# TensorE's order through two attention branches, written by hand in place of the planner's

## The chip, the cores and the metric

The kernel runs on one NeuronCore of a Trainium2 chip. The metric is device time in microseconds, from the first to the last instruction of one launch with what lies around it; the median of three runs is given. TensorE does the matrix products, VectorE, ScalarE and GpSimd (POOL in the rows) the elementwise work, and SyncE (SP) issues most DMAs.

## The reference, cut to what matters

Two layers of a decoder trunk over 1024 tokens of width 1024. In each layer one input projection of the normalised x feeds three branches, whose gated sum goes through an output projection.

```python
h = _rms(x, norm_g[l])
proj = h @ w_in[l]
# differential attention: 4 heads, two score maps of 64 each, causal
q = _partial_rope(_rms(q.reshape(B, S, DA_HEADS, 2, DA_QK_DIM), q_g), cos, sin)
k = _partial_rope(_rms(k.reshape(B, S, DA_HEADS, 2, DA_QK_DIM), k_g), cos, sin)
p = jax.nn.softmax(sc, axis=-1)
wdiff = p[:, :, 0] - lam * p[:, :, 1]
o = _rms(o, subln_g) * (1.0 - lam_init)          # o = wdiff @ v, then * silu(z)
# recurrent branch (RWKV-7): a scan over time
# memory cross-attention: 4 heads of 128, 256 memory tokens, softmax(q km) vm * silu(z)
gates = jax.nn.sigmoid(gate_logits.reshape(B, S, N_BRANCH, D_MODEL))
merged = jnp.sum(gates * branch_proj, axis=2)
x = x + merged @ w_out[l]
```

## The kernel before

Activations lie transposed, channels on partitions and tokens on the free axis. The input projection is cut into 65 column tiles of 128 channels a layer. A tile is two halves of 512 tokens; a half is 24 matmuls (8 blocks of the contraction, three products each, since weights and activations are split into a high and a low part). `project` (L220) computes one tile: `weight` (L198) loads 512 KB on SP's queue, ScalarE makes the high part, GpSimd the low part; then, for each half, 24 matmuls into a tile of the pool `pj` (two buffers) and a function `take` that reads it out. Work that needs TensorE again, such as sums over channels, is put on a list by `put_off` and runs when the next half has been taken; `run_later` empties the list at once.

The stages of a layer follow one another: the projections of the recurrent branch; its scan (`rwkv_run`), in which TensorE's order is written by hand and the tiles of a list (16 gate tiles and 8 SiLU tiles) are put in between by `fill`; cross attention; differential attention; merge; output projection. In the two attentions the order on every engine is a planner's, which goes by its own costs and by the order of the program. There `cross_prepare` (L818) projects the queries of the next head while `cross_run` (L838) runs one, and `diff_prepare` (L879) projects k, q and v of the next head (norm, spread of the norm over the tokens, rotation) while `diff_run` (L935) runs one. `FC` and `FD` say behind which heads a gate tile is projected (one in cross attention, one after each of the four heads of the other); one more follows. That makes 22 of 24 gate tiles, which are stored to `g_d` and loaded again in `merge`; `merge` projects the other two itself.

A head of differential attention goes through eight tiles of 128 queries. `scores(t)` makes both score maps in the pool `pg` (three buffers), takes the maximum on VectorE and the exponential on ScalarE, which frees the buffer; `finish(t)`, one tile later, combines the two maps on VectorE, transposes the result through the pool `pa` (tag "a", two buffers), copies it out and multiplies it with v. At the end `ov` is normalised and transposed once more. The sums, the spread norm (`ps_rb`) and v's transposes go through the pool `pu` (one buffer). The ring `dsn` has two buffers, which the rotation of k and q and the copy of v (L924) share.

Lines of helpers in the profile: L171 and L174 are VectorE's or GpSimd's two-operand operations, L178 ScalarE's high part, L214 every matmul of `project`, L249 a transpose, L269 the token sums in three parts ("sq", "rest").

Of the kernel before, what the change touches and what calls it, by code (L numbers as in the profile page):

```python
# [19 lines left out]
P = 128  # L20
# [36 lines left out]
FC, FD = (0, 1, 0, 0), (1, 1, 1, 1)  # L57

F_0, F_INV, F_H, F_U, F_S, F_END = 40, 140, (18, 8), 7, 6, (72, 72)
EARLY = 16  # L60
# [3 lines left out]
LAG = 1  # L64
# [66 lines left out]
def trunk(ctx, tc, io, out, layers=DEPTH, dump=None):  # L131
# [89 lines left out]
    def project(h, l, j, take, eng=None):  # L221
        w = weight(io["w_in"][l, j], eng)
        for hf in range(2):
            ps = pj.tile([P, 512], F32, name="ps_pj", tag="pj")
            product(ps, w, h, NK, slice(0, P), half(hf))
            old = later[:]
            later.clear()
            take(hf, ps)
            new = later[:]
            later.clear()  # L230
            for n, then in old:
                if n > 1:
                    later.append((n - 1, then))
                else:
                    then()
            later.extend(new)

    later = []

# [18 lines left out]
    def token_sums3(mp, ss, sq, rhs, bufs=2, eng=None):  # L258
# [6 lines left out]
        def sums(first):  # L265
# [7 lines left out]
    def spread(ps, col, n, c):  # L273
# [3 lines left out]
        nc.scalar.copy(bv, col.rearrange("p (j c) -> p j c", c=c).unsqueeze(3).to_broadcast([P, n, c, P // c]))  # L277
        for j in range(n):
            transpose(ps[:, j * P:(j + 1) * P], b[:, j * P:(j + 1) * P])
# [165 lines left out]
    def dense(h, l, items):  # L445

        def steps():
            ahead = weight(io["w_in"][l, items[0][0]])
            for t, (j, take) in enumerate(items):
                w = ahead  # L450
                ahead = weight(io["w_in"][l, items[t + 1][0]]) if t + 1 < len(items) else None
                for hf in range(2):
                    ps = pj.tile([P, 512], F32, name="ps_pj", tag="pj")
                    n = 0
                    for k in range(NK):
                        for a, b in ((0, 0), (0, 1), (1, 0)):
# [3 lines left out]
                            if n == 3 * NK:  # L460
                                take(hf, ps)
                            yield
        return steps()
# [149 lines left out]
    def rwkv_run(l, ch, dc, sts, gen):  # L613
# [3 lines left out]

        def fill(n):
            for _ in range(n):
                next(gen, None)  # L620
# [193 lines left out]
        fill(F_END[0])  # L814
        finish(yn, 3)
        fill(F_END[1])
        for _ in gen:
            pass  # L818


    def cross_prepare(l, q, h, mp, i):
        qT = mp.tile([P, S], F32, name="cq", bufs=2)
        ss = pu.tile([P, 512], F32, name="ps_ss", tag="u")
        es = mp.tile([P, NT], F32, name="ces", bufs=2)

        def take(hf, ps):
            sq = mp.tile([P, 512], F32, name="sq", bufs=2)
            nc.scalar.copy(qT[:, half(hf)], ps)
            nc.scalar.activation(sq, ps, AF.Square)  # L829
            sums = token_sums3(mp, ss[:, hf * 4:], sq, onesb)  # L830

            def then():
                sums(hf == 0)
                if hf == 1:
                    rsqrt(es, ss[:, :NT], NT, 1.0 / P, EPS, post=P ** -0.5)
            put_off(then)
        project(h, l, T_CAQ + i, take)
        return qT, es  # L838

    def cross_run(mp, kT, vm, i, qT, es):  # L840
# [3 lines left out]
        for t2 in range(4):  # L844
            ps = pg.tile([P, 512], F32, name="ps_c", tag="g")
            for u in range(2):
                t = t2 * 2 + u
                nc.tensor.matmul(ps[:, u * M:u * M + M], qT[:, t * P:t * P + P], kT[:, i, :], start=True, stop=True)
# [4 lines left out]
            stt(mx, mx, -1.0, es[:, t2 * 2:t2 * 2 + 2], ALU.mult, ALU.mult)  # L853
            e = mp.tile([P, 2, M], F32, name="ce", bufs=2)
            for u in range(2):
                t = t2 * 2 + u
                nc.scalar.activation(e[:, u, :], pv[:, u, :], AF.Exp, scale=es[:, t:t + 1], bias=mx[:, u:u + 1],
                                     accum_out=ls[:, u:u + 1])
            nc.vector.reciprocal(ls, ls)
            for u in range(2):  # L860
                nc.vector.tensor_scalar(e[:, u, :], e[:, u, :], ls[:, u:u + 1], None, op0=ALU.mult)
            pt = pa.tile([P, 512], F32, name="ps_t", tag="a")
# [3 lines left out]
            for m in range(2):  # L866
                nc.vector.tensor_copy(pT[m][:, t2 * 256:t2 * 256 + 256], pt[:, m * 256:m * 256 + 256])
        for hf in range(2):
# [3 lines left out]
            y = mp.tile([P, 512], F32, name="ce", bufs=2)  # L872
            ttv(y, ps, zs[:, half(hf)], ALU.mult)
            nc.gpsimd.dma_start(y_d[2, i][:, half(hf)], y)
        run_later()


    def diff_prepare(l, q, h, mp, rope, i):

        cos, sin, rot = rope  # L880
        es = mp.tile([P, NT, 2], F32, name="des", bufs=2)
        qk = {}

        def rest(n, g, ss):
            if n == "q":
                rsqrt(es.rearrange("p t c -> p (t c)"), ss[:, :16], 16, 1.0 / 64, EPS, post=0.125)
            else:
                r = mp.tile([P, 16], F32, name="dkr", bufs=2)
                rsqrt(r, ss[:, :16], 16, 1.0 / 64, EPS)
                for hf in range(2):  # L890
                    rb = pu.tile([P, 512], F32, name="ps_rb", tag="u")
                    spread(rb, r[:, hf * 8:hf * 8 + 8], 4, 2)
                    ttv(g[:, half(hf)], g[:, half(hf)], rb, ALU.mult)
# [9 lines left out]
        for n, tl in (("k", T_DAK), ("q", T_DAQ)):  # L903
            g = mp.tile([P, S], F32, name="d" + n, bufs=1)
            ss = pu.tile([P, 512], F32, name="ps_ss", tag="u")

            def take(hf, ps, n=n, g=g, ss=ss):
# [3 lines left out]
                sums = token_sums3(mp, ss[:, hf * 8:], sq, hindb)  # L911

                def then():
                    sums(hf == 0)
                    if hf == 1:
                        rest(n, g, ss)
                put_off(then)
            project(h, l, tl + i, take)
            qk[n] = g
        v = mp.tile([P, NT, P], F32, name="dv", bufs=2)  # L920

        def take_v(hf, ps):
# [3 lines left out]
            def then(vt=vt):  # L926
                pt = pu.tile([P, 512], F32, name="ps_t", tag="u")
                for j in range(4):
                    transpose(pt[:, j * P:j * P + P], vt[:, j * P:j * P + P])
                nc.scalar.copy(v[:, hf * 4:hf * 4 + 4, :].rearrange("p t d -> p (t d)"), pt)  # L930
            put_off(then)
        project(h, l, T_DAV + i, take_v)
        return qk, v, es

    def diff_run(l, q, te, mp, identb, negb, kl, i, qk, v, es, beside):  # L935
# [19 lines left out]
        def scores(t):  # L955
# [3 lines left out]
            for c in range(2):  # L959
# [18 lines left out]
                stt(mx[:, 0:1], mx[:, 0:1], -1.0, es[:, t, c:c + 1], ALU.mult, ALU.mult)  # L978
                e = mp.tile([P, S], F32, name="de", bufs=4)
# [9 lines left out]
        def finish(t, ee, ll):  # L989
# [9 lines left out]
            for b in range(nb):  # L999
# [17 lines left out]
        for t in range(NT):  # L1017
            pend.append((t, *scores(t)))
            if len(pend) > LAG:
                finish(*pend.pop(0))  # L1020
            if t == 2:
                run_later()
        for u in pend:
            finish(*u)
        beside()
# [125 lines left out]
    for l in range(layers):  # L1151
# [4 lines left out]
        def fill(n):  # L1156
            for _ in range(n):
                g = queue.pop(0)
                early.add(g)
                project(h, l, T_GATE + g[0] * 8 + g[1], take_gate(*g))  # L1160
        with tc.tile_pool(name="st", bufs=1) as sp:
# [14 lines left out]

            silus = [(T_CAZ + i, take_silu(2, i)) for i in range(4)] + [(T_DAZ + i, take_silu(0, i)) for i in range(4)]
            items = []
            for i in range(EARLY):
# [71 lines left out]
```

## Time and profile before

| | us |
|---|---|
| median of the runs | 2776.12 |
| lowest and highest of 3 runs | 2769.37, 2777.94 |
| profiled execution, its own time | 2769.06 |
| its span, first to last instruction | 2767.3 |

The rows below come from that one profiled execution. Times in rows are in us; names are those of the program, out<-in. A number in brackets at the end of a row of the timeline is how long the engine sat idle before it, and what ended that. The granted clock (PEclk) is 1.00 when TensorE has its full rate.

### The profile page before, as it was taken

To read this page: it belongs to the slowest core of one execution; us is meant where nothing else is said; L and a number is where in the kernel's file an instruction comes from. 1 tells how busy PE (TensorE), PEld (TensorE's weight loads), DVE (VectorE), ACT (ScalarE), POOL (GpSimd) and SP (SyncE) were. 2 spreads that over 40 slices of the span, in tenths; PEclk is the share of its full clock that TensorE was granted. 3 is DMA by queue.
4 is the path that set the end of the run, shared out by engine and by line. 5 is a ranking of instruction groups with operands and counts; after the bars stand their busy time and mean duration, and the time that the engine had idled before them with its cause. 6 is when DMAs were issued, how large, how long until landed. Compare 5 with 4: busy or idle time off the path is not lost. (4 is left out here: it accounts for less than half of the span.)

```text
span 2767.3 us, 40395 instructions
## 1 busy us (share of the span) xinstructions
PE 2643.5 (96%) x15686; PEld 2144.8 (78%) x15686; DVE 1690.4 (61%) x3427; ACT 986.6 (36%) x1927; POOL 816.0 (29%) x716
## 2 busy tenths in 40 slices
PE   7799999999999999999999999999999999999999
PEld 7788788888876777777877778888887677777787
DVE  3748557557356777845556765656735577774552
ACT  4444322212232555722234432222223345573221
POOL 3445522232312222122234652123231222212210
PEclk8799999999999999999999999999999999999999
DMA  4323442322322112155352345223232211114534
GB/s 156 105 92 122 149 146 96 104 88 64 117 75 77 39 54 58 50 182 165 118 163 75 115 133 180 88 85 101 79 106 81 80 43 54 51 53 171 171 108 150
DMA packets 94479, 286.91 MB, mean 104 GB/s; under 512 B 12368, under 2 KB 19152, under 8 KB 91856
## 3 DMA queue, kind: packets, MB, share of 16 engines
q1 hardware_dynamic: 67088, 196.24, 23.5%
q0 software_dynamic: 25024, 83.90, 7.8%
q10 hardware_dynamic: 2176, 4.19, 0.4%
q8 instruction: 123, 2.02, 0.3%
q14 instruction: 68, 0.56, 0.1%
HBM read 198.31 MB, written 83.89 MB: 102 GB/s over the span
## 5 line engine op out<-in xcount | busy, mean ns | idle before, releaser
L171 POOL TENSOR_TENSOR w_lo<-w_raw,w_hi 128x1024 fp32r<-128x1024 f32 x170 | 421.2, 2478 | 937.5 <-ACT w_hi L178 891.1
L214 PE MATMUL ps_pj<-hh,w_hi 128*128 128x512 f32 x1568 | 634.5, 405 | 1.2 <-ACT hh L178 1.2
L214 PE MATMUL ps_pj<-hl,w_hi 128*128 128x512 f32 x1568 | 625.6, 399 | 1.2 <-DVE hl L171 1.2
L214 PE MATMUL ps_pj<-hh,w_lo 128*128 128x512 f32 x1568 | 622.9, 397 | 0.6 <-DVE w_lo L171 0.6
L178 ACT ACTIVATE w_hi<-w_raw 128x1024 fp32r<-128x1024 f32 x202 | 213.9, 1059 | 670.4 <-PE ps_pj L214 242.9
L214 PEld LDWEIGHTS ps_pj<-hl,w_hi 128*128 128x128 f32 x1568 | 298.1, 190 | 62.4 <-issue 4.3
L214 PEld LDWEIGHTS ps_pj<-hh,w_lo 128*128 128x128 f32 x1568 | 297.9, 190 | 61.7 <-issue 1.4
L214 PEld LDWEIGHTS ps_pj<-hh,w_hi 128*128 128x128 f32 x1568 | 297.7, 190 | 61.1 <-issue 2.9
L457 PE MATMUL ps_pj<-hh,w_hi 128*128 128x512 f32 x768 | 308.1, 401 | 0.0
L457 PE MATMUL ps_pj<-hl,w_hi 128*128 128x512 f32 x768 | 306.4, 399 | 0.0
L457 PE MATMUL ps_pj<-hh,w_lo 128*128 128x512 f32 x768 | 304.9, 397 | 0.0
L457 PEld LDWEIGHTS ps_pj<-hh,w_hi 128*128 128x128 f32 x768 | 146.5, 191 | 30.5
L457 PEld LDWEIGHTS ps_pj<-hh,w_lo 128*128 128x128 f32 x768 | 146.3, 190 | 30.4
L457 PEld LDWEIGHTS ps_pj<-hl,w_hi 128*128 128x128 f32 x768 | 146.5, 191 | 29.4
L1080 PE MATMUL ps_b<-yh,w_hi 128*128 128x512 f32 x384 | 147.5, 395 | 9.5 <-ACT yh L178 9.5
L1080 PE MATMUL ps_b<-yl,w_hi 128*128 128x512 f32 x384 | 152.7, 400 | 2.3 <-DVE misc L342 1.2
L1080 PE MATMUL ps_b<-yh,w_lo 128*128 128x512 f32 x384 | 150.5, 395 | 0.0
L981 ACT ACTIVATE de<-ps_d,dmx,des 128x512 f32<-128x512 f32 (+2 forms) x192 | 127.7, 670 | 50.7 <-DVE dmx L174 44.1
L171 DVE TENSOR_TENSOR rest<-sq 128x512 f32<-128x512 f32 x48 | 65.7, 1369 | 111.5 <-ACT sq L829 82.2
L974 DVE TENSOR_REDUCE dmx<-ps_d 128x1 f32<-128x512 f32 (+2 forms) x192 | 103.9, 551 | 23.1 <-PE ps_d L973 19.6
L442 POOL DMA_DIRECT2D g_d<-z_t x88 | 49.0, 557 | 213.3 <-ACT z_t L441 130.0
L171 DVE TENSOR_TENSOR inv_u<-inv_l,inv_x 128x126 f32<-128x126 f32 (+22 forms) x248 | 96.3, 388 | 16.4 <-ACT inv_l L670 9.6
(297 smaller groups left out, 4507.3 us busy)
## 6 DMA issues: line engine op xcount, KB each, us to landing
w_raw<-in_w_in_dram SPq DMA_DIRECT2D x130, 512.0 KB
g_d<-z_t POOLq DMA_DIRECT2D x88, 256.0 KB, 4.7
tg<-g_d SPq DMA_DIRECT2D x88, 256.0 KB
w_raw<-in_w_out_dram SPq DMA_DIRECT2D x32, 512.0 KB
z_d<-z_t POOLq DMA_DIRECT2D x48, 256.0 KB, 3.0
w_raw<-in_w_branch_dram SPq DMA_DIRECT2D x24, 512.0 KB
yr<-y_d SPq DMA_DIRECT2D x24, 512.0 KB
w_raw<-in_w_mem_dram SPq DMA_DIRECT2D x16, 512.0 KB
```

The costliest lines, as they stand in the source:

```text
L171: (eng or nc.vector).tensor_tensor(o, a, b, op=op)
L178: nc.scalar.activation(hi, src, AF.Copy)
L214: nc.tensor.matmul(ps, w[a][:, k, cols], act[b][:, k, toks], start=n == 0, stop=n == 3 * nk - 1)
L442: nc.gpsimd.dma_start(g_d[n, d][:, half(hf)], tg)
L457: nc.tensor.matmul(ps, w[a][:, k, :], h[b][:, k, half(hf)], start=n == 0, stop=n == 3 * NK - 1)
L974: nc.vector.tensor_reduce(mx[:, b:b + 1], ps[:, :n], axis=AX.X, op=ALU.max)
L981: nc.scalar.activation(e[:, b * 512:b * 512 + n], ps[:, :n], AF.Exp, scale=es[:, t, c:c + 1], bias=mx[:, 0:1], accum_out=ls[:, b:b + 1])
L1080: nc.tensor.matmul(pb, wb[a][:, i, (d % 2) * P:(d % 2) * P + P], b[i][:, half(hf)], start=k3 == 0, stop=k3 == 11)
```

## The change

In both attentions TensorE's order is now the program's. One list of column tiles (`Dense`) goes through the scan, cross attention and differential attention; `fill(n)` issues the next n matmuls of the list, up to a limit, and `until` issues all up to a tile. The constants say how many stand behind each step: `C_S`, `C_T`, `C_E` in cross attention, `D_S`, `D_M`, `D_T`, `D_E` in the other. The token sums, the spread of k's norm and v's transposes run when the next half tile has been taken. The queries of cross attention are projected two heads ahead; k, q, v and one gate tile of the next head lie inside each head of differential attention (192 matmuls), two gate tiles inside the last one, whose fills are halved. The spread norm and v's transposes move from `pu` to `pa`. The scan has 15 gate tiles instead of 16, 23 gates are early instead of 22, and the last fills of the scan are 60 and then what is left.

```diff
-F_0, F_INV, F_H, F_U, F_S, F_END = 40, 140, (18, 8), 7, 6, (72, 72)
-EARLY = 16
+F_0, F_INV, F_H, F_U, F_S, F_END = 40, 140, (18, 8), 7, 6, 60
+EARLY = 15
+C_S, C_T, C_E = 7, 3, 6
+D_S, D_M, D_T, D_E = (6, 8, 8, 10, 8, 8, 8, 8), (12, 6), 3, (12, 20)
...
+    class Dense:
+        def __init__(self, h, l):
+            self.items, self.done, self.limit, self.gen = [], 0, 0, self.steps(h, l)
...
+            for t, (j, take) in enumerate(self.items):
+                w = ahead or weight(io["w_in"][l, j])
+                ahead = weight(io["w_in"][l, self.items[t + 1][0]]) if t + 1 < len(self.items) else None
...
                             if n == 3 * NK:
-                                take(hf, ps)
+                                taken(take, hf, ps)
+                                self.done = t + hf
                             yield
...
+        def fill(self, n):
+            for _ in range(n):
+                if self.done < self.limit:
+                    next(self.gen)
+
+        def until(self, n):
+            while self.done < n:
+                next(self.gen)
...
+        ee = []
+        for t2 in range(4):
+            ee.append(scores(t2))
+            fill(C_S)
+            if t2:
+                turn(t2 - 1, ee[t2 - 1])
+                fill(C_T)
+        fill(C_E)
+        turn(3, ee[3])
+        fill(C_E)
...
+                bs = [spread_by_tokens(r[:, hf * 8:hf * 8 + 8], 4, 2) for hf in range(2)]
+
+                def then():
+                    for hf in range(2):
+                        rb = pa.tile([P, 512], F32, name="ps_rb", tag="a")
+                        for j in range(4):
+                            transpose(rb[:, j * P:(j + 1) * P], bs[hf][:, j * P:(j + 1) * P])
+                        ttv(g[:, half(hf)], g[:, half(hf)], rb, ALU.mult)
+                    rotate(n)
+                put_off(then)
...
-            def then(vt=vt):
-                pt = pu.tile([P, 512], F32, name="ps_t", tag="u")
+            def then():
+                pt = pa.tile([P, 512], F32, name="ps_t", tag="a")
...
                     last = b == nb - 1
+                    if c and b:
+                        fill(D_M[1])
...
+                if c == 0 and nb == 2:
+                    fill(D_M[0])
                 e = mp.tile([P, S], F32, name="de", bufs=4)
...
+            fill(D_T)
             po = pa.tile([P, 512], F32, name="ps_o", tag="a")
...
             pend.append((t, *scores(t)))
-            if len(pend) > LAG:
+            fill(D_S[t])
+            if t:
                 finish(*pend.pop(0))
...
+        fill(D_E[0])
+        finish(*pend.pop(0))
         rsqrt(oss, oss, NT, 1.0 / P, EPS, tag="ds")
         ttv(ov, ov, oss.unsqueeze(2).to_broadcast([P, NT, P]), ALU.mult)
+        fill(D_E[1])
...
+            unit = prepare_head(0)
+            dense.until(n_da[0])
+            for i in range(4):
+                ahead = prepare_head(i + 1) if i < 3 else None
+                dense.limit = n_da[i + 1]
+                diff_run(l, q, te, mp, identb, negb, kl, i, unit, dense.fill if i < 3 else lambda n: dense.fill(n // 2))
+                dense.until(n_da[i + 1])
+                unit = ahead
             run_later()
```

## Rows read from the trace of the kernel before

**Rows 1.** The page, part 1: busy time, share and instructions.

```profile
PE 2643.5 (96%) x15686; PEld 2144.8 (78%) x15686; DVE 1690.4 (61%) x3427; ACT 986.6 (36%) x1927; POOL 816.0 (29%) x716
```

**Rows 2.** Windows, differential attention: us; PE, PEld, DVE, ACT, POOL busy; PEclk; DMA; GB/s.

```profile
868.00:942.00 74.00, 66.91 (x362) 51.97 (x363) 44.50 (x90) 26.42 (x45) 24.09 (x15) 0.93 0.22 64
942.00:1200.00 258.00, 247.95 (x1430) 194.62 (x1429) 199.24 (x557) 155.90 (x405) 53.48 (x39) 0.99 0.19 59
...
2186.00:2262.00 76.00, 67.69 (x383) 52.29 (x381) 46.05 (x92) 28.40 (x46) 26.67 (x17) 0.98 0.22 67
2262.00:2516.00 254.00, 245.22 (x1401) 192.56 (x1402) 195.95 (x549) 152.61 (x400) 50.07 (x38) 0.97 0.18 55
```

**Rows 3.** TensorE's waits, 868:942 and 2186:2262: total us, times, longest.

```profile
PE ps_t L249 <- ACT dsn L924: 4.8, 3, 3.0
PE ps_ss L269 <- ACT sq L910: 2.6, 1, 2.6
...
PE ps_t L249 <- ACT dsn L924: 4.3, 3, 3.0
```

**Rows 4.** TensorE's waits, 740:868 (the first row stands in both layers).

```profile
PE ps_ss L269 <- DVE rest L171: 3.5, 4, 0.9
PE ps_t L249 <- DVE ce L861: 1.6, 1, 1.6
```

**Rows 5.** TensorE's waits, 942:1200 and 2262:2516.

```profile
PE ps_d L968 <- ACT de L981: 6.3, 4, 2.0
PE ps_t L249 <- ACT dsn L924: 1.8, 3, 0.6
...
PE ps_d L968 <- ACT de L981: 5.9, 3, 2.0
PE ps_t L249 <- ACT dsn L924: 1.5, 2, 0.9
```

**Rows 6.** Timeline of TensorE: start, duration; first and last of two streams.

```profile
795.54 0.40 PE L214 MATMUL ps_pj<-hl,w_hi 128*128 128x512 f32 x1
...
801.22 0.39 PE L214 MATMUL ps_pj<-hh,w_lo 128*128 128x512 f32 x1
...
873.96 0.63 PE L214 MATMUL ps_pj<-hh,w_lo 128*128 128x512 f32 x1
...
877.37 0.55 PE L214 MATMUL ps_pj<-hl,w_hi 128*128 128x512 f32 x1
```

**Rows 7.** Timeline, all engines, start of the first layer's first head.

```profile
942.77 2.36 POOL L171 TENSOR_TENSOR w_lo<-w_raw,w_hi 128x1024 fp32r<-128x1024 f32 x1 [5.99 <-PE ps_d L973]
...
943.00 2.15 DVE L174 SCALAR_TENSOR_TENSOR dmx<-dmx,des 128x1 f32<-128x1 f32 x1
...
943.10 0.48 PE L214 MATMUL ps_pj<-hh,w_hi 128*128 128x512 f32 x1
...
945.78 0.44 PE L968 MATMUL ps_d<-dkh,dqs 128*128 128x256 f32 x1 [1.97 <-ACT de L981]
```

**Rows 8.** Timelines of TensorE and ScalarE: k's norm spread, v's copy.

```profile
884.10 0.66 PE L249 MATMUL ps_rb<-con,spread 128*128 128x128 f32 x4
...
899.11 0.59 ACT L924 COPY dsn<-ps_pj 128x512 f32<-128x512 f32 x1 [10.42 <-DVE dk L171]
```

**Rows 9.** Timeline of VectorE: a step of cross attention, maximum to scaled probabilities.

```profile
785.24 0.67 DVE L852 TENSOR_REDUCE cmx<-ps_c 128x2 f32<-128x512 f32 x1
...
788.71 0.60 DVE L861 TENSOR_SCALAR ce<-ce,cls 128x256 f32<-128x256 f32 x2
```

**Rows 10.** Timeline of TensorE: first layer's merge; second layer's last head and merge.

```profile
1208.89 0.98 PE L1080 MATMUL ps_b<-yh,w_hi 128*128 128x512 f32 x3 [1.58 <-ACT yh L178]
...
2507.87 2.05 PE L1011 MATMUL ps_o<-dv,dwT 128*128 128x128 f32 x16
...
2514.60 1.07 PE L249 MATMUL ps_t<-con,dov 128*128 128x128 f32 x8 [0.33 <-DVE dov L171]
...
2528.38 0.97 PE L1080 MATMUL ps_b<-yh,w_hi 128*128 128x512 f32 x3 [2.45 <-ACT yh L178]
```

More of the change, by code (lines that the diff above doesn't have):

```diff
@@ L225, in project, with taken @@
             product(ps, w, h, NK, slice(0, P), half(hf))
-            old = later[:]
-            later.clear()
-            take(hf, ps)
[L229 to L236, printed above, removed]
-    later = []
+            taken(take, hf, ps)
+    later = []
+    def taken(take, hf, ps):
+        old = later[:]
+        later.clear()
+        take(hf, ps)
+        new = later[:]
+        later.clear()
+        for n, then in old:
+            if n > 1:
+                later.append((n - 1, then))
+            else:
+                then()
+        later.extend(new)
     def put_off(then, n=1):
@@ L443, in take_gate, with add, steps @@
         return take
[L445 to L451, printed above, removed]
+    class Dense:
+        def __init__(self, h, l):
+            self.items, self.done, self.limit, self.gen = [], 0, 0, self.steps(h, l)
+        def add(self, j, take):
+            self.items.append((j, take))
+            return len(self.items)
+        def steps(self, h, l):
+            ahead = None
+            for t, (j, take) in enumerate(self.items):
+                w = ahead or weight(io["w_in"][l, j])
+                ahead = weight(io["w_in"][l, self.items[t + 1][0]]) if t + 1 < len(self.items) else None
                 for hf in range(2):
@@ L843, in cross_run, with scores @@
         pT = [mp.tile([P, S], F32, name="dwT", bufs=2) for _ in range(2)]
-        for t2 in range(4):
+        def scores(t2):
             ps = pg.tile([P, 512], F32, name="ps_c", tag="g")
@@ L871, in cross_run, with diff_prepare, rotate @@
                 nc.tensor.matmul(ps, vm[:, i, m, :], pT[m][:, half(hf)], start=m == 0, stop=m == 1)
-            y = mp.tile([P, 512], F32, name="ce", bufs=2)
+            y = mp.tile([P, 512], F32, name="cy", bufs=2)
             ttv(y, ps, zs[:, half(hf)], ALU.mult)
             nc.gpsimd.dma_start(y_d[2, i][:, half(hf)], y)
-        run_later()
-    def diff_prepare(l, q, h, mp, rope, i):
+    def diff_prepare(l, q, mp, rope):
         cos, sin, rot = rope
[L881 to L893, printed above, removed]
+        x = dict(es=mp.tile([P, NT, 2], F32, name="des", bufs=2), k=mp.tile([P, S], F32, name="dk", bufs=1),
+                 q=mp.tile([P, S], F32, name="dq", bufs=1), v=mp.tile([P, NT, P], F32, name="dv", bufs=2))
+        def rotate(n):
+            g = x[n]
             for c in (0, 64):
@@ L1154, in trunk, with gate, lazy @@
         early = set()
[L1156 to L1160, printed above, removed]
+        def gate():
+            g = queue.pop(0)
+            early.add(g)
+            return T_GATE + g[0] * 8 + g[1], take_gate(*g)
+        dense = Dense(h, l)
+        units = {}
+        def lazy(*name):
+            return lambda hf, ps: units[name](hf, ps)
+        silus = [(T_CAZ + i, take_silu(2, i)) for i in range(4)] + [(T_DAZ + i, take_silu(0, i)) for i in range(4)]
+        for i in range(EARLY):
+            dense.add(*gate())
+            if i % 3 == 0 and i:
+                for _ in range(min(2, len(silus))):
+                    n_rw = dense.add(*silus.pop(0))
+        assert not silus
+        n_ca, n_da = [], []
+        for i in range(4):
+            n_ca.append(dense.add(T_CAQ + i, lazy("c", i)))
+        for i in range(2):
+            n_ca.append(dense.add(*gate()))
+        for i in range(4):
+            for n, tl in (("k", T_DAK), ("q", T_DAQ), ("v", T_DAV)):
+                dense.add(tl + i, lazy(n, i))
+            n_da.append(dense.add(*gate()))
+        dense.add(*gate())
+        n_da.append(dense.add(*gate()))
         with tc.tile_pool(name="st", bufs=1) as sp:
@@ L1175, in trunk @@
                 run_later()
-            silus = [(T_CAZ + i, take_silu(2, i)) for i in range(4)] + [(T_DAZ + i, take_silu(0, i)) for i in range(4)]
-            items = []
-            for i in range(EARLY):
-                g = queue.pop(0)
-                early.add(g)
-                items.append((T_GATE + g[0] * 8 + g[1], take_gate(*g)))
-                if i % 3 == 0 and i:
-                    items += [silus.pop(0) for _ in range(min(2, len(silus)))]
-            assert not silus
-            with tc.tile_pool(name="ch", bufs=1) as ch, tc.manual_schedule(engines={mybir.EngineType.PE}):
-                rwkv_run(l, ch, dc, sts, dense(h, l, items))
```

143 lines of the change are left out of this document (74 added, 69 removed).

## The prediction

> **What bounds the kernel now.** I read the page first: TensorE is busy 96% of a span of 2767.3 us, VectorE 61% [rows 1]. [...] The gain of a new order on TensorE can only come from three things: time in which it waits, time at the low clock, and matmuls that start late after a change of kind. It executes the same matmuls before and after: 23 gate tiles are computed early in place of 22, one fewer in the merge.
>
> Then I took the stages one by one, by the granted clock [rows 2] and by TensorE's own waits.
>
> - Cross attention: 3.5 us in each layer for the token sums' second part ("rest"), 1.6 us in the first for the last head's probabilities [rows 4]: 8.6 us.
> - Start of the differential attention (868 to 942, 2186 to 2262 us): 4.8 and 4.3 us for v's copy, 2.6 us in each layer for the squares [rows 3]: 14.3 us. Clock 0.93 and 0.98 [rows 2]: 74 x 0.07 + 76 x 0.02 = 6.7 us.
> - The heads themselves: 6.3 and 5.9 us until a score buffer comes free, 1.8 and 1.5 us for v's copy [rows 5]: 15.5 us. Clock 0.99 and 0.97: 258 x 0.01 + 254 x 0.03 = 10.2 us.
> - First branch products of the merge: 1.58 and 2.45 us [rows 10]: 4.0 us.
>
> So some 59 us in 2767 lie where the new order can reach them. The reader should see that the low clock follows the waits: the slow matmuls at 873.96 us come behind the wait for the squares, so a shortened wait pays twice.
>
> **The change part by part.** *Sums put off by half a tile (start of differential attention, cross).* Half a tile is 24 matmuls, 24 x 0.227 = 5.4 us. The squares and the "rest" (waits of 2.6 and 0.9 us at most [rows 3, 4]) are covered by that; what would take the cover away is VectorE or ScalarE being more than 5 us late. Of the 21.0 us at the start of the differential attention not all goes. The copy of v shares a ring of two buffers ("dsn") with the rotation of k and q, and the new order leaves that ring as it is. Before, the spread of k's norm began at 884.10 and v's copy at 899.11, after ScalarE had stood idle 10.42 us [rows 8]: 15.0 us. The new order puts the spread behind q's second half and v's first transposes two halves later, 10.9 us: 4.1 us short, and the second copy waited 3.0 us before already [rows 3]. So up to 7.1 us a layer stays. At the other end nothing stays, because q's norm on VectorE now comes half a tile later, out of the way of k's rotation. I take the middle, 3.5 us a layer: 21.0 - 7 = **14 us won** (7 to 21).
>
> *Cross attention in steps of 7, 3 and 6 matmuls.* From the maximum to the last scaled probabilities took 785.24 to 788.71 + 0.60 = 4.1 us [rows 9]. [...] Of 8.6 us I keep half: **4 us won** (0 to 8.6). Weights come one tile ahead in either version, and the queries' list crosses the stages, so no load stands newly in front of TensorE; nothing on SP's or POOL's queue is moved past another but the store and load of one more gate, hidden as 22 are now.
>
> *The heads.* Before: 15.5 + 10.2 = 25.7 us. At a head's start VectorE's tiny 128x1 operation took 2.15 us, as long as POOL's split of the next weights (2.36 us) ran beside it, and TensorE then stood 1.97 us for the score buffer [rows 7]. The new order begins a tile at the same place, so that split stays there; but 6 matmuls lie between the first and second scores where 2 lay, 4 x 0.227 = 0.9 us more: 1.07 us stays in six heads, and 1.7 us in the two last heads, whose fills are halved: 9.9 us. New are three things. The norm of k for the next head now goes through the pool of the transposes ("a", two buffers), just ahead of five transposes that need both: VectorE's product, some 0.7 us each, makes that 1.2 us, six times: 7 us. Ahead of a head's final transposes the chain from the last output product to the scaled output takes 2507.87 + 16 x 0.11 to 2514.60, that is 4.9 us [rows 10]; 20 matmuls (4.5 us) leave 0.4 us six times, 10 matmuls (2.3 us) in the last heads 2.6 us twice: 7.6 us. Low clock behind the last two: 1 us. Together 25.5 us: **0 won**. Lower end: if the waits inside scores and transposes that I count as covered each cost another 0.25 us (some eight a head, 64 in all), 16 us lost. Upper end: if the first scores and the pool cost nothing, 17 us won.
>
> *Merge.* On the timeline the planner had drawn the merge's first gate into the last head; by hand it comes behind it, 48 x 0.227 = 10.9 us in front of the first branch product, more than the 1.58 and 2.45 us [rows 10]: **4 us won** (0 if the loads move with it).
>
> *Changes of kind.* A projection matmul behind another kind took 0.48 us where its neighbours took 0.39 [rows 6, 7]: 0.09 us. By the code, projections are cut into some 11 pieces a head in cross attention and 34 in the other. For three pieces a head more than the planner's, 16 heads: 48 x 0.09 = **4 us lost** (0 to 4).
>
> *The end of the recurrent branch.* 12 fewer matmuls before its last output (2.7 us): the chain there was not among TensorE's waits, so nothing; if that cover were gone, at most 2.7 us a layer.
>
> Sum: 14 + 4 + 0 + 4 - 4 = **18 us** off the profiled execution's 2769.06 us (span 2767.3 and 1.8 around it): 2751. The median of the runs shown, 2776.12, lies 7.1 us above that execution, so the median I forecast is 2776 - 18 = **2758 us**.
>
> **The rivals.** *Nearly all waits go.* The code spreads 192 projection matmuls over each head; VectorE is busy 199 of 258 us in the heads [rows 2], so there is slack for it. Against: the splits on POOL still hit VectorE. Price, all upper ends: 21 + 8.6 + 17 + 4 = 51 us: 2725.
>
> *The waits only move (no change).* VectorE has 77% of the heads' time filled now and would have a shorter time; each head start keeps its whole 1.97 us (8 x 1.97 = 15.8 in place of 9.9), the start of differential attention its 7.1 us a layer, and cross attention wins nothing: 18 - 6 - 7 - 4 = 1 us won, 2775. For it: the same split beside the same operation [rows 7]. [...]
>
> *Slower: ScalarE stands at v's copy.* It is one queue in order: at 899.11 it had been idle 10.42 us with the copy at its head [rows 8], and then nothing else wanted it. In the new order v's two copies fall amid the scores of the seventh and eighth query tiles, with exponentials behind them that free the score buffers. From the second block of scores to the need of the first one's buffer lie 18 matmuls and one score block, some 4.6 us; what follows the scale needs some 2.5 us (from the end of the held-up operation, 943.00 + 2.15, to TensorE's release at 945.78 it was 0.63 us for 128 columns [rows 7]; I estimate four times that for two blocks of 512). So it decides from 2.1 us of standing. With 5.5 us it costs 3.4 us at 12 copies (two in each of the three heads that prepare a next one, two layers): 41 us, so 2758 + 41 = 2799. Against: a half tile takes some 9 us inside a head, twice the 5.4 us that made the ring so late here. [...]
>
> **How the numbers follow.** A measurement of this kernel can tell about 0.3%, 8.3 us, from no change. My forecast 0.50, its own range 2744 to 2768 (18 us, give or take what one or two terms can miss); nearly all waits go 0.15; only moved 0.18; slower 0.17. So faster 0.65, same 0.18, slower 0.17. The range of 8 in 10 runs from just above the best case, 2728, to 2787, which cuts off the worse half of the slower case and the tail of the best.
>
> **What would show it.** Right: no TensorE wait for "sq" or "rest"; clock near 1.00 at the start of the differential attention; at head starts waits of about 1 us for the score buffer; waits of "rb" or "t" tiles on VectorE once a head; the largest single wait left ahead of the last head's final transposes. Wrong: waits of TensorE for v's copy or for exponentials in the middle of a head add up to more than 20 us, or VectorE's share in the heads rises with TensorE's time unchanged.

## The result: slower by 1.2%, and the profile after

The changed kernel takes 2806.86 us (median of four runs, 2805.74 to 2810.43) against 2774.78 us of the kernel before beside it: a ratio of 1.012 with a 95% interval of 1.0101 to 1.0139. I had forecast 2758 us, faster. The profiled execution took 2806.0 us.

The page after, part 1, answers to [rows 1]:

```profile
PE 2643.8 (94%) x15686; PEld 2151.2 (77%) x15686; DVE 1716.5 (61%) x3427; ACT 993.1 (35%) x1927; POOL 817.3 (29%) x720
```

TensorE is busy as long as before (2643.5 us then), and the span has grown from 2767.3 to 2804.2 us: the whole loss is idle time of TensorE. TensorE's waits by stage say where. First cross attention and the start of the differential attention (757 to 904 us, and 2100 to 2246 in the second layer, where the two rows of cross attention stand again), then the heads of the first layer (904 to 1224); total us, times, longest:

```profile
PE ps_t L255 <- ACT dsn L971: 2.1, 2, 1.9
PE ps_t L255 <- DVE ce L885: 0.6, 1, 0.6
PE ps_t L255 <- DVE ces L176: 0.5, 1, 0.5
...
PE ps_t L255 <- ACT dsn L971: 3.4, 2, 1.9
```

```profile
PE ps_d L1017 <- ACT de L1032: 17.4, 7, 4.6
PE ps_o L1063 <- DVE dwT L1059: 10.3, 8, 2.0
PE ps_o L1063 <- ACT dwT L1057: 4.5, 6, 1.3
PE ps_o L1063 <- DVE dcf L1045: 0.4, 1, 0.4
PE ps_t L255 <- DVE de L176: 0.3, 1, 0.3
PE ps_t L255 <- DVE dov L173: 0.3, 1, 0.3
```

The waits for the squares and the "rest" [rows 3, 4] are gone. In the heads TensorE waits 33.2 us, and 33.3 in the second layer. Before it was 9.6 and 8.7 us: the rows of [rows 5] and 1.5 and 1.3 us of smaller waits. Windows after, start and heads of both layers, with the columns of [rows 2]:

```profile
858.00:902.00 44.00, 41.90 (x226) 33.83 (x225) 30.20 (x51) 19.39 (x32) 17.31 (x12) 0.96 0.28 84
902.00:1224.00 322.00, 287.62 (x1635) 227.41 (x1634) 230.19 (x599) 170.48 (x421) 65.61 (x47) 0.98 0.18 54
2200.00:2244.00 44.00, 40.62 (x227) 32.82 (x227) 29.30 (x51) 19.14 (x32) 17.27 (x12) 1.00 0.28 85
2244.00:2566.00 322.00, 287.61 (x1636) 227.38 (x1635) 229.47 (x592) 170.54 (x421) 66.08 (x47) 0.98 0.18 55
```

How the two kinds of wait arise shows on the timeline of the first head, which the next two heads repeat: waits of 2.0, 1.2 and 4.55 us at the same three places in the six heads that prepare a next one, some 46 of the 66.5 us in both layers. A wait of 2.0 us at the product with v:

```profile
923.83 2.40 POOL L173 TENSOR_TENSOR w_lo<-w_raw,w_hi 128x1024 fp32r<-128x1024 f32 x1 [17.09 <-ACT w_hi L180]
924.02 2.83 DVE L173 TENSOR_TENSOR rest<-rest 128x512 bf16<-128x512 f32 x1
...
927.70 0.78 ACT L1032 ACTIVATE de<-ps_d,dmx,des 128x512 f32<-128x512 f32 x1 [3.57 <-DVE dmx L176]
928.47 0.45 ACT L1032 ACTIVATE de<-ps_d,dmx,des 128x128 f32<-128x128 f32 x1
929.04 0.16 DVE L173 TENSOR_TENSOR dls<-dls 128x1 f32<-128x1 f32 x1 [1.38 <-ACT de L1032]
929.31 0.67 DVE L1059 COPY dwT<-ps_t 128x512 f32<-128x512 f32 x1
930.04 1.16 PE L1063 MATMUL ps_o<-dv,dwT 128*128 128x128 f32 x8 [1.99 <-DVE dwT L1059]
```

The copy itself takes 0.67 us, no longer than the three matmuls (0.68 us) that stand in front of the product. It is late because VectorE stood 2.83 us in an operation beside GpSimd's split, and because a small addition that waits for ScalarE's exponentials is queued in front of it. And a wait of 4.55 us for a score buffer, in the eighth query tile:

```profile
956.67 0.39 PE L1017 MATMUL ps_d<-dkh,dqs 128*128 128x512 f32 x1
957.62 0.69 DVE L173 TENSOR_TENSOR dq<-dq,att 128x512 f32<-128x512 f32 x1
...
959.68 0.68 DVE L1023 TENSOR_REDUCE dmx<-ps_d 128x1 f32<-128x512 f32 x1
...
961.77 1.28 DVE L1023 TENSOR_REDUCE dmx<-ps_d 128x1 f32<-128x512 f32 x2
...
963.47 2.57 POOL L173 TENSOR_TENSOR w_lo<-w_raw,w_hi 128x1024 fp32r<-128x1024 f32 x1 [2.41 <-ACT w_hi L180]
963.87 2.18 DVE L176 SCALAR_TENSOR_TENSOR dmx<-dmx,des 128x1 f32<-128x1 f32 x1
...
966.09 0.78 ACT L1032 ACTIVATE de<-ps_d,dmx,des 128x512 f32<-128x512 f32 x1 [1.75 <-DVE dmx L176]
967.01 0.49 PE L1017 MATMUL ps_d<-dkh,dqs 128*128 128x512 f32 x1 [4.55 <-ACT de L1032]
```

The scores ran from 956.1; their maxima start at 959.68 and 961.77, behind the next head's rotation, and then the 128x1 operation that the exponential needs takes 2.18 us beside the next split. The two windows around the wait (columns as above) show what it costs beyond itself: TensorE's granted clock is 0.57 in the mean of the 4 us behind it. The matmuls from 968.39 to 970.52 start every 0.43 us, at a granted clock of 0.50; at 1.00 they start every 0.227 us, the figure in which the prediction counts its covers (26 starts from 795.54 to 801.22 us, kernel before).

```profile
962.00:967.00 5.00, 0.45 (x2) 0.02 (x1) 4.92 (x7) 3.25 (x7) 2.57 (x1) 1.00 0.00 2
967.00:971.00 4.00, 3.99 (x11) 2.95 (x12) 3.78 (x10) 3.69 (x8) 0.00 (x0) 0.57 0.40 131
```

### The profile page after: what moved, and what is told of

Its sections match the earlier page's. It is cut to its first block, busy times and chain, and to the rows that moved or that the text cites. A ratio compares the mean times of both kernels' runs of the same rounds, so it can differ in the third digit from the quotient of the medians.

```text
span 2804.2 us, 40373 instructions
## 1 busy us (share of the span) xinstructions
PE 2643.8 (94%) x15686; PEld 2151.2 (77%) x15686; DVE 1716.5 (61%) x3427; ACT 993.1 (35%) x1927; POOL 817.3 (29%) x720
## 5 line engine op out<-in xcount | busy, mean ns | idle before, releaser
L1063 PEld LDWEIGHTS ps_o<-dv,dwT 128*128 128x128 f32 x576 | 70.8, 192 | 52.3 <-DVE dwT L1059 27.7
L1063 PE MATMUL ps_o<-dv,dwT 128*128 128x128 f32 x576 | 81.1, 286 | 31.2 <-DVE dwT L1059 20.6
```

The costliest lines, as they stand in the source:

```text
L1063: nc.tensor.matmul(po[:, :P], wT[:, j, :], v[:, j, :], start=j == 0, stop=j == t)
```

## The experiments

The kernel before, run beside each group of these kernels, had medians between 2772.2 and 2777.6 us, so I compare by ratio to it (95% interval in brackets); the change stands at 1.012. Unless said otherwise the base is the changed kernel.

### Which stage, and what lateness

**e1, hand order in cross attention only.**

```diff
-        with tc.tile_pool(name="dte", bufs=1) as te, tc.tile_pool(name="atp", bufs=2) as mp, \
-                tc.manual_schedule(engines={mybir.EngineType.PE}):
+        with tc.tile_pool(name="dte", bufs=1) as te, tc.tile_pool(name="atp", bufs=2) as mp:
```

> The changed kernel, but in the differential attention the planner orders TensorE again; cross attention stays in hand order, the list of tiles, the put-off sums and the pools stay as changed. Theory (the loss sits in the hand order inside the heads, where TensorE now waits 35 us for exponentials and 30 us for the copies of the transposed weights): the time falls to 2755 to 2775 us and TensorE's waits for dwT are gone. Rival (what the heads do, k, q and v spread through one list and the pool of the transposes shared, is at fault whoever orders it): 2795 to 2810 us.

2765.8 us, 0.9971 [0.9952, 0.9991]: the whole loss and a little more comes back, so it sits in the hand order inside the differential attention, not in the list, the pools or the put-off sums. Of the 43.8 us of span, 24.3 are waits for exponentials and 16.4 are busy time of TensorE (2643.8 to 2627.4 us for the same matmuls; the mean granted clock of the whole execution rises from 0.977 to 0.983). Half of what I expected of the rows was wrong: the copies' waits stay (12.6 and 16.8 us, 29.8 in all before the edit); those for exponentials fall from 34.8 to 10.5. The planner drew the last tile's scores ahead of the product (954.25 us here), and VectorE takes their maxima at once, in front of the rotation:

```profile
957.22 0.68 DVE L1023 TENSOR_REDUCE dmx<-ps_d 128x1 f32<-128x512 f32 x1
...
957.91 0.68 DVE L1023 TENSOR_REDUCE dmx<-ps_d 128x1 f32<-128x512 f32 x1
...
958.59 0.68 DVE L173 TENSOR_TENSOR dq<-dq,att 128x512 f32<-128x512 f32 x1
```

**e2, hand order in the differential attention only:** the same edit at cross attention's two pools.

> The changed kernel, but cross attention is ordered by the planner and only the differential attention by hand. Theory: the heads keep their waits (35 us for exponentials, 30 us for the copies) and cross attention gives back what it won, so 2805 to 2825 us. Rival (the hand order in cross attention carries a share of the loss): below 2800 us.

2812.1 us, 1.014 [1.0115, 1.0164]: the loss stays.

**e3, no low part in the heads** (TensorE multiplies the high part in its place).

```diff
+        if low:
             split(hi, lo, raw, eng or nc.gpsimd)
+        else:
+            nc.scalar.activation(hi, raw, AF.Copy)
+            lo = hi
```

> The changed kernel without the low part of the weights of the 14 tiles that are projected inside the heads of each layer: GpSimd's subtraction is left out there and the high part stands in for the low one, so TensorE does the same number of matmuls and only their values change. Rival (collision: VectorE's operations take 2 to 3 us where GpSimd's split runs beside them, and the copies and exponentials behind them are late): the 4.6 us and 2.0 us waits go, 30 to 40 us less, 2765 to 2778 us. Theory (VectorE's queue in order holds the copies behind work that waits for ScalarE, and three matmuls cover too little): most of the waits stay, 2790 to 2803 us.

2761.4 us, 0.9959 [0.9941, 0.9976]: 45 us less, more than the collision theory gave. The copies' waits fall from 29.8 to 10.6 us and those for exponentials from 34.8 to 17.3.

**e4, more cover for the copies.**

```diff
-D_S, D_M, D_T, D_E = (6, 8, 8, 10, 8, 8, 8, 8), (12, 6), 3, (12, 20)
+D_S, D_M, D_T, D_E = (2, 2, 2, 2, 2, 2, 2, 2), (12, 6), 9, (12, 20)
```

> The changed kernel with nine projection matmuls in place of three between the transposes of the weights and the product with v (2.0 us of cover for 0.7), and two in place of 6 to 10 behind the scores; the sum of a head stays 192. Theory (the cover of the copies is too short by itself): the 30 us of waits for dwT fall below 8 us and the time to 2778 to 2790 us. Rival (VectorE is late by whole operations and the wait only moves on to the next score buffer): TensorE's waits for exponentials grow by what the copies' waits lose, 2797 to 2812 us.

2803.2 us, 1.0112 [1.0084, 1.014]: no difference that can be told from the change. TensorE's waits, whole run:

```profile
PE ps_d L1017 <- ACT de L1032: 52.2, 18, 6.6
PE ps_t L255 <- DVE de L176: 10.7, 10, 1.4
...
PE ps_o L1063 <- ACT dwT L1057: 1.3, 4, 0.4
PE ps_o L1063 <- DVE dwT L1059: 1.3, 6, 0.2
```

The 29.8 us at the product are 2.6 now, and stand at the score buffers and the transposes instead: the wait moved on, as the rival said.

### Order against collision

**e5, the product with v behind the first map of the next scores.**

```diff
+            def product_v():
                 po = pa.tile([P, 512], F32, name="ps_o", tag="a")
...
+            products.append(product_v)
...
+                if c == 0 and products:
+                    products.pop(0)()
                 if c == 0 and nb == 2:
                     fill(D_M[0])
```

> The changed kernel, TensorE still in hand order, but the product with v of a query tile comes behind the first map of the next tile's scores and not in front of it (where the planner put it when it ordered the heads). Theory (TensorE stands at the product for the copies with the next scores queued behind it, so their maxima come late, and VectorE's queue, which the planner orders by its own times, then has the next head's rotation in front of them): most of the 4.6 us waits go, 2770 to 2785 us. Rival (GpSimd's split beside VectorE alone): the waits stay, 2795 to 2808 us.

2779.1 us, 1.0021 [1.0004, 1.0039]: 28 us won. The waits for exponentials fall from 34.8 to 12.2 us; the copies' stay at 30.1. The edit is in TensorE's order alone, but the planner, which still orders VectorE, changed that engine's order with it: here the last tile's maximum goes ahead of the rotation, where it stood behind it in the changed kernel.

```profile
954.60 0.68 DVE L1023 TENSOR_REDUCE dmx<-ps_d 128x1 f32<-128x512 f32 x1
...
955.96 0.68 DVE L173 TENSOR_TENSOR dq<-dq,att 128x512 f32<-128x512 f32 x1
```

So the 28 us belong to both orders together.

**e6, the heads' low parts on VectorE.**

```diff
-                ahead = weight(io["w_in"][l, self.items[t + 1][0]]) if t + 1 < len(self.items) else None
+                ahead = weight(io["w_in"][l, self.items[t + 1][0]], nc.vector if t + 1 >= self.head else None) \
+                    if t + 1 < len(self.items) else None
```

> The changed kernel with the low part of the weights of the 14 tiles projected inside the heads made by VectorE and not by GpSimd. Collision theory: no small operation of VectorE takes 2 us any more, and the 14 x 1.3 us that it has in their place are less than the standing beside GpSimd's 14 x 2.4 us; 2770 to 2785 us. Rival (VectorE has too much to do in the heads, the collision is only a part of it): the time stays or grows, 2803 to 2825 us.

2775.9 us, 1.0008 [0.9994, 1.0022]: 31 us won. VectorE's groups (count | busy us, mean ns | idle), first the changed kernel, then this one:

```profile
L173 DVE TENSOR_TENSOR rest<-rest 128x512 bf16<-128x512 f32 x48 | 48.3, 1005 | 0.3
L176 DVE SCALAR_TENSOR_TENSOR dmx<-dmx,des 128x1 f32<-128x1 f32 x128 | 41.7, 333 | 2.1
L173 DVE TENSOR_TENSOR w_lo<-w_raw,w_hi 128x1024 fp32r<-128x1024 f32 x32 | 40.3, 1260 | 4.5 <-ACT w_hi L180 4.5
```

```profile
L173 DVE TENSOR_TENSOR w_lo<-w_raw,w_hi 128x1024 fp32r<-128x1024 f32 x60 | 74.5, 1242 | 5.2 <-ACT w_hi L180 5.2
...
L173 DVE TENSOR_TENSOR rest<-rest 128x512 bf16<-128x512 f32 x48 | 36.1, 752 | 0.3
L176 DVE SCALAR_TENSOR_TENSOR dmx<-dmx,des 128x1 f32<-128x1 f32 x128 | 25.8, 205 | 2.0
```

VectorE takes on 28 splits (34.2 us), and is busy 1706.5 us in all where it was 1716.5: its other operations lose 44 us. The operation in front of the last tile's exponentials, 2.18 us long in the changed kernel, takes 0.16 us:

```profile
962.10 0.16 DVE L176 SCALAR_TENSOR_TENSOR dmx<-dmx,des 128x1 f32<-128x1 f32 x1
```

Still TensorE waits 21.2 us for exponentials, 2.7 us at the longest, so the split was not the whole of the 4.55 us.

**e7, e1 and e6 together.**

> Both at once: the planner orders TensorE in the differential attention (2765.8 us so far), and VectorE makes the low part of the weights of the 14 tiles inside the heads. If order and collision are two separate causes, their gains add up: 2740 to 2755 us. If the planner's order already hides what the collision costs, 2760 to 2775 us.

2719.4 us, 0.9814 [0.9799, 0.9829]: 87 us below the change, more than 41 and 31 together. Neither case of mine had that. Read the other way, the hand order in the heads costs 41 us with the splits on GpSimd and some 56 with them on VectorE (2775.9 against 2719.4).

**e8, maxima ahead of the rotation** in VectorE's queue (an order of issue, no wait).

```diff
+                if t == NT - 1 and c == 0:
+                    while turns:
+                        tc.add_manual_dep(turns.pop().ins, top.ins.name, mybir.DependencyInfo(
+                            mybir.DependencyClass.NoSync, mybir.DependencyReason.DATA), reason="max first")
```

> The changed kernel, but on VectorE the four operations of the rotation of the next head's q are queued behind the two maxima of the eighth query tile's first map; TensorE's order is untouched. If the rotation in front of the maxima makes the 4.6 us waits, they fall by some 2 us each in six heads and the low clock behind them goes: 2785 to 2796 us. If they come from the collision or from the late product, 2800 to 2808 us.

2801.0 us, 1.0117 [1.0091, 1.0143]: no difference. The waits for exponentials fall only from 34.8 to 30.5 us, the longest from 4.6 to 3.9. The rotation in front of the maxima, which the timeline shows, does not cost by itself; but the split held the same 128x1 operation again (2.30 us), so this run does not tell what the rotation costs without the split.

### The same mend in both kernels

**f1, the kernel before with the heads' low parts on VectorE.**

```diff
-            project(h, l, tl + i, take)
+            project(h, l, tl + i, take, nc.vector if i else None)
```

(and likewise for v and the five gate tiles).

> The kernel before, with one edit: VectorE and not GpSimd makes the low part of the weights of the 14 tiles that are projected among the heads of each layer. If the planner's order had absorbed what GpSimd's split costs VectorE (so that only the hand order pays for it), the time stays at 2765 to 2777 us. If the kernel before paid for it just as well, 2725 to 2750 us, and then it isn't what the change lost.

2747.9 us, 0.9898 [0.9873, 0.9922]: the kernel before paid for the split just as well, some 28 us. So this collision is not what the change lost.

**f2, e5 and e6 together,** in hand order.

> The changed kernel in hand order with both mends: the product with v behind the first map of the next scores (2779 us alone) and the low part of the heads' weights on VectorE (2776 us alone). If the two mends take away different waits: 2806.9 - 28 - 31 = 2748 us. If together they leave TensorE next to nothing to wait for, as where the planner orders the heads: 2715 to 2730 us. If both take away the same waits: 2765 to 2775 us.

2727.2 us, 0.9835 [0.9806, 0.9865]: 80 us below the change, where 28 and 31 add to 59. The heads of this kernel, with the columns of [rows 2]:

```profile
900.90:1185.00 284.10, 276.40 (x1634) 224.76 (x1633) 220.70 (x612) 169.28 (x421) 33.24 (x34) 1.00 0.20 62
2200.20:2484.00 283.80, 276.34 (x1633) 224.76 (x1633) 219.80 (x605) 169.29 (x421) 33.08 (x34) 1.00 0.20 61
```

The same matmuls as in the changed kernel's 322 us, in 284: TensorE is busy 11.2 us a layer less, at a clock of 1.00, and idle 26.7 us less.

Where the order decides is seen in the ten us from the last query tile's first score matmul in the first head: the changed kernel, e6 and this one.

```profile
956.10:966.10 10.00, 6.35 (x32) 4.75 (x30) 9.93 (x22) 6.37 (x13) 3.86 (x2) 1.00 0.00 1
```

```profile
954.30:964.30 10.00, 7.32 (x36) 5.40 (x35) 9.92 (x25) 8.02 (x17) 1.29 (x1) 1.00 0.00 1
```

```profile
948.30:958.30 10.00, 9.97 (x52) 7.77 (x51) 10.00 (x30) 7.59 (x16) 2.58 (x2) 1.00 0.01 2
```

VectorE has no free time there (9.92 to 10.00 us), whoever makes the low parts. What differs is how much TensorE can do meanwhile: 6.35, 7.32 and 9.97 us.

**f3, e7 with 9 more low parts a layer on VectorE** (cross attention, first head).

> The fastest so far (planner's order in the heads, 14 low parts a layer on VectorE, 2719.4 us), with the low parts of the tiles of cross attention and of the first head's k, q and v on VectorE as well, 9 more a layer. If VectorE's operations are stretched there too and TensorE waits for them: 2708 to 2716 us. If TensorE's wait there is only that for v's copy: 2717 to 2723 us.

2717.6 us, 0.9796 [0.9771, 0.9821]: not to be told from e7. These two are the fastest kernels here, 2% below the kernel before.

**f4, fills dealt to the large tiles:** D_S (4, 4, 4, 4, 12, 12, 12, 12).

> The changed kernel with the same 64 matmuls behind the scores of a head dealt otherwise: 4 behind each of the first four query tiles and 12 behind each of the last four, in place of 6 to 10 and 8. If the waits come from too little work of TensorE at the large tiles, where VectorE is late: 2780 to 2795 us. If any fixed places do as badly, because what is late moves on along VectorE's queue: 2800 to 2815 us.

2796.0 us, 1.0073 [1.0049, 1.0097]: some 13 us, between the two cases.

### Which place in the order

**g1, the copy ahead of the additions** in VectorE's queue, by the device of e8.

```diff
+                            if (t + 1, c) in adds:
+                                tc.add_manual_dep(adds[t + 1, c].ins, copy.ins.name, ...
```

> The changed kernel; on VectorE the two small additions of the exponentials' sums of a query tile (which wait for ScalarE) are queued behind the copy of the transposed weights of the tile before. TensorE's order is untouched. If the copy's place in VectorE's queue makes TensorE's waits at the product: the 20.6 us behind VectorE's copies fall below 8 us and the time to 2780 to 2793 us. If what is late only moves on to the next score buffer, as with more cover: 2797 to 2808 us.

2792.1 us, 1.0059 [1.0034, 1.0084]: some 17 us. TensorE's waits, whole run:

```profile
PE ps_d L1017 <- ACT de L1032: 35.2, 14, 4.6
...
PE ps_o L1068 <- DVE dwT L1059: 4.4, 10, 0.6
```

VectorE's copies cost 4.4 us of waiting in place of 20.6, and nothing moved to the score buffers (34.8 before this edit). So the copy's place behind those additions is one cause by itself.

**g2, e1 with the scores held behind the product.**

```diff
+                    if products:
+                        tc.add_manual_dep(first.ins, products[-1].ins.name, ...
```

> The kernel whose heads the planner orders (2765.8 us), with one thing held: the scores of a query tile stay behind the product with v of the tile two before, as in the hand order; all else of TensorE's order stays free. If that one place in the order is the loss: 2793 to 2808 us. If the hand order loses through its fixed fills, which the planner may still move here: 2765 to 2778 us.

2764.3 us, 0.9965 [0.9949, 0.9981]: no loss. The theory that I had drawn from e5, that this place is the fault, falls. Under that constraint the planner moved projection matmuls: ten in place of three between the sixth query tile's transposes and its product (first and last of the ten, and the product, which does not wait):

```profile
959.68 0.48 PE L475 MATMUL ps_pj<-hh,w_lo 128*128 128x512 f32 x1
...
961.82 0.39 PE L475 MATMUL ps_pj<-hh,w_lo 128*128 128x512 f32 x1
962.05 1.24 PE L1066 MATMUL ps_o<-dv,dwT 128*128 128x128 f32 x9
```

**g3, f2 with all 23 low parts on VectorE.**

> The hand order with the product behind the first map of the next scores, and the low parts of all 23 tiles of both attentions on VectorE (2727 us with 14 of them). If the 9 others cost TensorE as little as in the planner's kernel, 2722 to 2729 us; if the hand order covers the copies better once nothing stretches VectorE at the start, 2708 to 2720 us.

2734.1 us, 0.9846 [0.982, 0.9872]: not to be told from f2; the start of the stage holds no more.

**h1, the planner's numbers in hand order.**

```diff
+D_S, D_M, D_T, D_E = (6, 8, 8, 10, 8, 8, 8, 3), ((11, 6), (11, 6), (9, 6), (5, 14)), \
+    (3, 3, 4, 4, 4, 10, 3, 3), (12, 19)
```

> The hand order with its steps as they are, but with the numbers of matmuls that the planner chose under the same order of scores and product (2764.3 us): among others 10 in place of 3 ahead of the product of the sixth query tile, 14 in place of 6 ahead of the last block of scores, 3 in place of 8 behind the eighth tile's scores; 192 a head as before. If the numbers at these places are the loss: 2763 to 2778 us. If what the planner also moves (transposes ahead of the last block of scores, single matmuls between them) carries it: 2790 to 2808 us.

2788.4 us, 1.005 [1.0028, 1.0071]: some 19 of the 42 us that g2 won. The waits for exponentials stay at 31.5 us (20.7 in g2).

**h2, one of these places:** ten in place of three ahead of the sixth tile's product.

> The changed kernel with one place of the eight altered: ahead of the product of the sixth query tile, which stands in front of the last tile's scores, 10 matmuls in place of 3; 5 fewer behind the last tile's scores and 2 fewer ahead of its transposes. If the 1.2 us wait at this product is what makes the maxima late and with them the 4.6 us waits at the last block: these fall by half and the time to 2775 to 2790 us. If not, 2797 to 2810 us.

2797.3 us, 1.0083 [1.0056, 1.011]: some 10 us, and the longest wait for exponentials is still 4.4 us. The 1.2 us wait ahead of the scores is not what makes the 4.6 us waits.

**h3, h1 with the heads' low parts on VectorE.**

> The hand order with the planner's numbers, and the low parts of the 14 tiles in the heads on VectorE (2775.9 us with the numbers as changed, 2727.2 us with the product later). If the numbers are the loss: 2715 to 2730 us. If they only suit the lateness that GpSimd's split makes: 2755 to 2775 us.

2759.8 us, 0.9942 [0.9922, 0.9962]: the second case. Without the split in the way these numbers win some 18 us again, but some 30 us less than moving the product (f2).

## Why the prediction was wrong

**The step that failed** is the term of the heads, "0 won", and in it the sentence on "the waits inside scores and transposes that I count as covered". The prediction gives no working for that. Against the length of one operation the covers do suffice (three matmuls, 0.68 us, for a copy of 0.67 us), and I bounded the error at 16 us, 0.25 us a wait, with no row for the 0.25. TensorE's waits in the heads went from 18.3 to 66.5 us, 48 more, and the clock fell behind the longest (0.57, 0.60 and 0.57 in the mean of the 4 us behind the first layer's three waits of some 4.55 us; 1.00, 0.58 and 1.00 behind its three of some 1.95 us). What I had not followed is the queue in front of each operation: the copy waits behind additions that wait for ScalarE (g1: 17 us), the maxima and exponentials behind all that VectorE has to do at the end of a head, where it is full. I had read VectorE's share over the whole of the heads (77%), which hides that stretch.

**What the hand order lost.** Three facts, each from a comparison of runs. The loss is the order's: with the planner ordering the same program it is gone (e1). It is not the split's: with the split on VectorE the hand order still stands above the kernel before by as much (1.0008 against 0.9898, some 30 us; f1, e6). It is not one place's: moving the product wins 28 us, yet holding the product where it was costs nothing if the fills may move (e5, g2), and none of the fills and places in VectorE's queue that I altered gives more than 17 us (e4, e8, f4, g1, h2). Order and split do not simply add: both together give more than their sum (e7: 87 for 72; f2: 80 for 59). The windows under f2 fit all this: with VectorE full at a head's last tiles, TensorE stands unless scores were sent early or projection matmuls are left for that place, and a fixed order that does neither waits there in every head. In that stretch TensorE is busy 6.57 us in h1, 7.68 in g2, 9.14 in e1 and 9.58 in e5, with VectorE at 9.91 us or more in all four. That this is the whole of the loss isn't shown, and since the planner orders VectorE anew under each of TensorE's orders, no run separates the two orders in full. What carries the 24 us between h1 and g2 stays open: h1 took over the planner's numbers, not the transposes and single matmuls it had moved between the last tile's blocks.

**Term by term.** *Start:* forecast 14 us; the waits fell from 14.3 to 5.5 us and the low clock [rows 2] from 6.7 to some 1.8 (44 x 0.04), so 13.7. The copy of v kept the rest, near the forecast (5.5 for 7). *Cross:* forecast 4, half of the waits, an estimate of mine that no run shows; measured 6.4 (8.6 to 2.2). *The named terms of the heads:* too dear. The second and third head begin with waits of some 0.55 us (I had 1.07), the last with 1.24 (1.7). The spread of k's norm made no wait for the pool (I had 7 us), and the final transposes cost 0.6 us in all (I had 7.6). What I had named was covered; what I had counted as covered was the loss. *Merge:* forecast 4 us won; the waits at its branch products add up to 11.7 us before and 14.3 after, 2.6 lost. The step was wrong, too: the merge's first gate does not come behind the last head. The planner drew it in there in spite of the hand order, ahead of the last output product at 1208.50 us:

```profile
1202.58 0.40 PE L216 MATMUL ps_pj<-hh,w_hi 128*128 128x512 f32 x1
```

*Changes of kind* can't be told apart: TensorE's busy time is as before. In sum: heads 48 lost in waits and some 3 more at the low clock (12.9 for 10.2), start and cross 20 won, merge 2.6 lost, which makes 33 of the 37 us of span; the rest I can't place.

**The rivals.** The slower side happened, 7.9 us beyond that rival's 2799, but not by its mechanism. That ScalarE is one queue in order, the trace of the kernel before shows: it stood idle 0.43 us, until 451.55 us, for a result of VectorE, while an operation of the scan that ran behind it, at 454.07, had its input from 445.12 and its buffer from 447.51 us on. ScalarE did stand 3.64 us at a copy of v, with an exponential behind it (the copy starts at 953.38 us, the exponential at 953.99), but the exponentials that TensorE stands for longest wait for VectorE (the row at 966.09 us). I made no run that gives the copy a ring of its own, so its share in VectorE's lateness stays untested. "The waits only move" had named the split beside VectorE and underrated it: it was worth some 30 us to either kernel (e6, f1), and so is not the difference between them. The wrong-sign test that I had written down ("waits for exponentials in the middle of a head add up to more than 20 us") is what the profile shows.

**The good parts of the change were there.** With the low parts on VectorE in both kernels and the product later, the hand order is faster than the kernel before by 20.6 us (2727.2 against 2747.9, beside the same runs), near the 18 us that I forecast, but that is luck: the sum of the prediction has neither mend in it. Nor do the hand-ordered heads earn it, for with the planner's order in the heads the same program takes 2719.4 us (e7). What the change is worth without them and with the splits where they were is e1's 0.3%, some 8 us.

## What to carry to other kernels

When an order is fixed by hand, size each cover by when its input is ready in the trace, counting all that stands in front of it in its engine's queue, and not by how long one operation takes. Look for the short stretch in which another engine is full (here VectorE, 9.9 of 10 us at a head's last tiles, 77% over the heads), and see that the fixed order has work for that place. Test a collision in both kernels before it is blamed for the difference: here it cost both the same. More cover at the place where TensorE waits proves little: it may only move the wait (e4), so watch the sum of waits and not one row.

## What the hardware showed that I had not expected

Moving 28 splits from GpSimd (2.4 to 2.6 us each) to VectorE (1.24 us each) made VectorE less busy, not more: 1716.5 to 1706.5 us. A 128x1 operation that takes 0.16 us without the split (e6) ended, at 966.05 us, just when the split beside it ended (963.47 + 2.57), so its length was the rest of the split's and not its own; in the mean these operations take 333 ns beside GpSimd's splits and 205 ns without those of the heads. Other work of GpSimd does the same: beside a rotation product (953.97 + 1.27 us, changed kernel) a 128x16 operation of one input took 0.70 us, from 954.56 to the end of the product, where its successor at 955.51 took 0.16.
